# The first product of two feed forwards, by blocks in seven products instead of eight

## The chip, the cores and the metric

The kernel runs on one core of a Trainium2 chip. A time is the device time of one execution in microseconds (us). The kernel before took 2294.47 us (median of three runs, 2292.39 to 2301.81). The engines are named as in the profile: PE (TensorE: matrix products, with its weight loads as PEld), DVE (VectorE), ACT (ScalarE), POOL (GpSimd) and SP (SyncE, which here issues the transfers).

## The reference, cut to what matters

Two stacks of layers work on one array of 512 tokens by 1024 features in float32. The second stack has two layers, and each ends with a feed forward, which is all that the change touches:

```
h = rmsnorm(x, norm_g[i, 2]) * (1.0 + sc2) + sh2
y = jnp.square(jax.nn.relu(h @ ffn_w1[i])) @ ffn_w2[i]      # 1024 -> 4096 -> 1024
x = x + g2 * rmsnorm(y, norm_g[i, 3])
```

Layer 0 also has, beside its feed forward, to sum up the modulation (`c_act @ ada_w`) of layer 1.

## The kernel before

Float32 accuracy on PE comes from splitting. `split` (lines 191 and 192) writes a high part, rounded to fp32r, with a cast on ACT, and the rest with a subtraction on DVE; it reads two operands in SBUF there. `mm3` (lines 280 to 282) is then three matmuls: high by high, high by low, low by high. The transposed input of a feed forward lies in `XH` and `XL` (in the trace `xt_hi`, `xt_lo`): 8 blocks of 128 features by 512 tokens.

The 4096 hidden features are made in 8 chunks of 512. `up_first` makes chunk 0 in two halves of 256 tokens, as the tokens arrive. `up(c)` makes chunk c = 1 to 7: four weight pieces of 256 rows by 512 columns (2 KB per row), and for each of 4 groups of 128 features 8 times three matmuls of 512 columns, 96 in all. `act` takes each result through Relu and Square (ACT) and splits it into `H[c]`. `down(c)` multiplies two chunks with the second weight, 192 matmuls of 512 columns, and adds the result to `Y` (line 1290, DVE; for c = 0 a copy on ACT). The order is chunk 0, 1, down(0), 2, 3, down(2), 4, 5, down(4), 6, 7, and then `final_out` with the last two. So in each layer six chunks come in pairs (2, 3), (4, 5) and (6, 7), and chunk 1 comes right behind `up_first`.

The kernel is written with a layer that gives each engine its own list of instructions, sorted by a planner; an engine takes its list strictly in order. So an instruction that waits holds up all that stands behind it on its engine. Buffers come from two pools of slots: `mid` (4 KB per partition), divided into `w` for weights and `a` for the rest, and `small` (2 KB). A slot is given again in the order in which slots came free, so a transfer starts when the last reader of its slot is done. PSUM has 8 banks; `up` uses 0 to 3 for its four groups.

In the trace, POOL's only work near a feed forward is a power of a column (line 376), the reciprocal root that a block of 128 tokens needs twice: once when the residual is added, once when the new input is normed. The sums over `ada_w` (line 461) stand on DVE and wait for a transfer each.

Of the kernel before, what the change touches and what calls it, by code (L numbers as in the profile page):

```python
# [9 lines left out]
F32 = mybir.dt.float32  # L10
F32R = mybir.dt.float32r
# [5 lines left out]
P = 128  # L17
SEQ = 512
NB = SEQ // P
D = 1024  # L20
KD = D // P
# [9 lines left out]
def kernel(ctx: ExitStack, tc: tile.TileContext, inp: dict, out: bass.AP):  # L31
    nc = tc.nc
    V, S, G, T = nc.vector, nc.scalar, nc.gpsimd, nc.tensor
    mult, add, sub, amax, amin = ALU.mult, ALU.add, ALU.subtract, ALU.max, ALU.min
# [4 lines left out]
    class Ring:  # L39
        def __init__(self, items):  # L40
            self.items, self.i = items, 0
# [5 lines left out]
    def fixed(name, shape, dt=F32):  # L47
        return pool.tile([P] + list(shape), dt, tag=name, name=name)

    class Slots:  # L50
# [16 lines left out]
        def free(self, *tiles):  # L67
            for t in tiles:
                name, i = self.held.pop(t.name)
                self.idle[name].append(i)  # L70
# [14 lines left out]
    mid = Slots("mid", 4096, w=11, a=16)  # L85
    small = Slots("small", 2064, c=6, f=11, m=4)

    banks = [psum.tile([P, 512], F32, tag=f"bank{i}", name=f"bank{i}") for i in range(8)]
# [5 lines left out]
    XH = fixed("xt_hi", [KD, SEQ], F32R)  # L94
    XL = fixed("xt_lo", [KD, SEQ], F32R)
# [24 lines left out]
    def blk(i):  # L120
        return slice(i * P, (i + 1) * P)
# [67 lines left out]
    def split(hi, lo, src):  # L189

        S.copy(hi, src)  # L191
        V.tensor_sub(lo, src, hi.bitcast(F32))  # L192
# [4 lines left out]
    def w_piece(parts, nr=2):  # L197

        r, h, l = (mid.new("w", [nr, D // nr], dt) for dt in (F32, F32R, F32R))
        o = 0  # L200
        for ap in parts:
            n = ap.shape[1]
            nc.sync.dma_start(r[:, :, o : o + n], ap.rearrange("(k p) n -> p k n", p=P))
            o += n
        for i in range(nr) if by_tile[0] else (slice(0, nr),):
            split(h[:, i, :o], l[:, i, :o], r[:, i, :o])
        mid.free(r)
        return h, l
# [35 lines left out]
    class Turns:  # L244
# [18 lines left out]
        def need(self, key):  # L263

            while any(k == key for k, _, _ in self.steps):
                self.run()
# [12 lines left out]
    def mm3(o, lh, ll, rh, rl, start, stop):  # L279
        T.matmul(o, lhsT=lh, rhs=rh, start=start, stop=False)  # L280
        T.matmul(o, lhsT=lh, rhs=rl, start=False, stop=False)  # L281
        turns.passed(o, T.matmul(o, lhsT=ll, rhs=rh, start=False, stop=stop))  # L282
# [16 lines left out]
    def proj_feats(ws, ct, m=P, o=None, t=slice(0, SEQ)):  # L299

        if o is None:
            o = proj_bank.next()[:m, :]
        for k in range(KD):
            wh, wl = ws(k)
            mm3(o, wh[:, ct * P : ct * P + m], wl[:, ct * P : ct * P + m], XH[:, k, t], XL[:, k, t], k == 0, k == KD - 1)
        return o
# [4 lines left out]
    def dense(w, row0, nk, cols, term, tiles=(0, 1, 2, 3), nr=2):  # L311

        bs = {i: banks[n] for n, i in enumerate(tiles)}
        for k0 in range(0, nk, nr):
            r = slice(row0 + k0 * P, row0 + (k0 + nr) * P)
            h, l = w_piece([w[r, c0 : c0 + n] for c0, n in cols], nr)
            for i in tiles:
                for q in range(nr):
                    k = k0 + q
                    term(bs[i], i, k, h[:, q, :], l[:, q, :], k == 0, k == nk - 1)  # L320
            mid.free(h, l)
        return bs
# [7 lines left out]
    def of_out(o):  # L330
        return lambda b, tb, k, wh, wl, start, stop: mm3(b, *o(tb)(k), wh, wl, start, stop)

    def out_half(nk, o, ws):

        b = out_bank.next()
        for k in range(nk):
            mm3(b, *o(k), *ws(k), k == 0, k == nk - 1)
        return b

    def pair(name):  # L340

        t = mid.new(name, [2, 4, P], F32R)
        return t, t[:, 0, :, :], t[:, 1, :, :]
# [106 lines left out]
    def ada_sum(l, part):  # L450

        for k in range(KD):
            for hf in range(2):
                t = ada_in[0].next()
                c0 = part * D + hf * 512
                nc.sync.dma_start(t, inp["ada_w_2"][l, k * P : (k + 1) * P, c0 : c0 + 512])
                a, ck = ada_acc[hf], c_act[:, k : k + 1]
                if k == 0:
                    V.tensor_scalar(a, t, ck, None, op0=mult)
                else:  # L460
                    V.scalar_tensor_tensor(a, t, ck, a, op0=mult, op1=add)  # L461
# [756 lines left out]

    def final_out(o, w, row0, Y, row, then):

        acc = [tiny(2) for _ in range(NB)]
        ys = []
        for hf in range(2):
            ws = bs = None
            if hf == 0:
                bs = dense(w, row0, KD, [(0, 512)], of_out(o))
            else:
                ws = out_weight(w, row0, KD, hf)
            for tb in range(NB):
                b = out_half(KD, o(tb), ws) if ws else bs[tb]  # L1230
                if Y is None:
                    ys.append(small.new("f", [512]))
                    S.copy(ys[-1], b)
                else:
                    ys.append(Y[tb][hf])
                    V.tensor_add(ys[-1], ys[-1], b)
                mean_squares(acc[tb][:, hf : hf + 1], ys[-1], D)
                V.tensor_mul(ys[-1], ys[-1], row[hf])
                if hf == 1:
                    with tc.high_priority(100):  # L1240
                        res_block(tb, (ys[tb], ys[NB + tb]), acc[tb], row, then)
        ws.free()


    def ffn(l, then):
        w1, w2 = inp["ffn_w1_2"][l], inp["ffn_w2_2"][l]
        mid.share(w=15, a=12, front=True)
        small.share(c=6, f=11, front=True)
        H = {}

        def act(hi, lo, b, shape):
            t = small.new("c", [SEQ])
            S.activation(t, b, AF.Relu)
            S.activation(t, t, AF.Square)
            split(hi, lo, t.rearrange("p (c t) -> p c t", c=shape) if shape else t)
            small.free(t)

        def up(c):
            H[c] = Parts()
            bs = dense(w1, 0, KD, [(512 * c, 512)], by_feat)  # L1260
            for ct in range(4):
                act(H[c].hi[ct], H[c].lo[ct], bs[ct], None)

        def up_first():

            H[0] = Parts()
            ws = Weight(w1, 0, KD, [(0, 512)])
            for hf in range(2):
                need(2 * hf + 1)
                if hf:  # L1270
                    small.share(c=4, f=13)
                t = slice(hf * 256, hf * 256 + 256)
                for q in range(2):
                    b = proj_bank.next()
                    for i in range(2):
                        proj_feats(ws, 2 * q + i, o=b[:, i * 256 : i * 256 + 256], t=t)
                    act(H[0].hi.ts[q][:, :, t], H[0].lo.ts[q][:, :, t], b, 2)
            ws.free()

        def of(c, tb):  # L1280
            return lambda k: H[c + k // 4](k % 4, blk(tb))

        def down(c):
            for hf in range(2):
                bs = dense(w2, 512 * c, KD, [(512 * hf, 512)], of_out(lambda tb: of(c, tb)))
                for tb in range(NB):
                    if c == 0:
                        S.copy(Y[tb][hf], bs[tb])
                    else:
                        V.tensor_add(Y[tb][hf], Y[tb][hf], bs[tb])  # L1290
            H.pop(c).free()
            H.pop(c + 1).free()

        up_first()
        mid.share(w=15, a=12)
        Y = [[small.new("f", [512]) for _ in range(2)] for _ in range(NB)]
        up(1)
        ada_sum(l, 5)
        down(0)
        row = ada_row(l, 5)  # L1300
        parts = [0, 1, 3, 4] if l == 0 else []
        for c in range(2, 8):
            up(c)
            if parts and c > 2:
                ada_cols(1, parts.pop(0))
            if parts:
                ada_sum(1, parts[0])
            if c in (3, 5):
                down(c - 1)
        small.share(c=7, f=10)  # L1310
        final_out(lambda tb: of(6, tb), w2, 512 * 6, Y, row, then)
        for q in (H.pop(6), H.pop(7)):
            q.free()
        small.free(*row)
# [113 lines left out]
    ple(1, NextH(0, 0))  # L1428
    mlstm(NextH(0, 2))
    ffn(0, NextH(1, 0))  # L1430
    sgu(NextH(1, 2))
    ffn(1, Store())


# [31 lines left out]
```

## Time and profile before

| | us |
|---|---|
| median of three runs | 2294.47 |
| the profiled execution | 2298.11 |
| its span, first to last instruction | 2296.4 |
| PE busy | 2249.7 |
| DVE busy | 1290.5 |
| ACT busy | 923.8 |
| POOL busy | 101.1 |

The profile is one execution, 3.6 us above the median of the runs. Busy time is the union of an engine's instructions; a busy PE is not PE at its peak, because its matmuls overlap. What a matmul costs in a dense stretch is the distance from one start to the next: 192 matmuls of 512 columns stand in the 44.41 us from 2022.10 to 2066.51, which is 0.231 us each, though one matmul shows 0.39 us.

### The profile page before, as it was taken

Reading aid. Unit: us, or ns where it says so; the run is one execution under the profiler, and the core shown is the slowest. Engines: PE = TensorE matmul, PEld = TensorE weight load, DVE = VectorE, ACT = ScalarE, POOL = GpSimd, SP = SyncE. Lnnn points to the kernel's source line nnn. Section 1 sums busy time; section 2 is a strip of 40 time slices with the busy share of each in tenths; the row PEclk is TensorE's granted clock in tenths of the full one; section 3 lists DMA queues with packets and bytes.
Section 4 is the critical chain, followed back from the end, with each engine's and each line's share of the span. In section 5 each row is a group of like instructions: output and inputs, shape, how many; then the busy total and the mean of one; then the engine's idle time right before and its main releaser. Section 6 shows DMA issues by size and latency. Waiting matters only on the chain.

```text
span 2296.4 us, 27232 instructions
## 1 busy us (share of the span) xinstructions
PE 2249.7 (98%) x10248; PEld 1803.4 (79%) x10248; DVE 1290.5 (56%) x2466; ACT 923.8 (40%) x1728; POOL 101.1 (4%) x157
## 2 busy tenths in 40 slices
PE   8999999999999999999998999999999998999998
PEld 6787788787777777887777887778788887888887
DVE  5665755844895857843647525556646457323334
ACT  4333444334354544333445432414535234442423
POOL 0000000100000000100211000000002101000000
PEclk9999999999999999999999999999999999999999
DMA  5343434222222124224414625454233443332230
GB/s 171 111 136 103 144 91 132 84 61 65 85 72 74 37 88 158 77 66 124 154 50 143 194 92 165 147 184 147 65 120 107 127 149 109 120 100 92 92 101 37
DMA packets 145767, 251.03 MB, mean 109 GB/s; under 512 B 13787, under 2 KB 34483, under 8 KB 145635
## 3 DMA queue, kind: packets, MB, share of 16 engines
q1 hardware_dynamic: 145632, 249.29, 34.7%
q8 instruction: 80, 1.31, 0.2%
q14 instruction: 55, 0.43, 0.1%
HBM read 247.15 MB, written 2.10 MB: 109 GB/s over the span
## 4 chain that ended last, share of the span: by engine, by line
PE 84%; DVE 7%; DMA 5%; ACT 2%; issue 1%; POOL 1%; SPq 0%; DVEq 0%; POOLq 0%; ACTq 0%
PE bank L280 25%; PE bank L281 25%; PE bank L282 25%; DMA small<-in_ada_w_dram 4%; DVE small L461 2%; PE bank L988 2%; DVE mid L192 1%; PE bank L287 1%; POOL tiny_c L376 1%; PE bank L1167 1%; PE bank L1172 1%; PE bank L1003 1%; PE bank L1391 1%; DVE x_res L521 0%; DMA mid<-in_gla_w_in_dram 0%
## 5 line engine op out<-in xcount | busy, mean ns | idle before, releaser
L192 DVE TENSOR_TENSOR mid<-mid,mid 128x512 fp32r<-128x512 f32 (+2 forms) x488 | 437.6, 916 | 623.0 <-ACT mid L191 550.5
L191 ACT CAST mid<-mid 128x512 fp32r<-128x512 f32 (+2 forms) x488 | 377.6, 799 | 854.4 <-PE bank L282 307.7
L280 PE MATMUL bank<-xt_hi,mid 128*128 128x512 f32 (+1 forms) x1216 | 471.7, 389 | 10.7 <-ACT xt_hi L191 9.6
L281 PE MATMUL bank<-xt_lo,mid 128*128 128x512 f32 (+1 forms) x1216 | 469.8, 386 | 4.2 <-DVE xt_lo L192 4.2
L282 PE MATMUL bank<-xt_hi,mid 128*128 128x512 f32 (+1 forms) x1216 | 468.9, 386 | 0.0
L280 PE MATMUL bank<-mid,mid 128*128 128x512 f32 x1032 | 410.1, 397 | 2.7 <-DVE small L1290 1.2
L281 PE MATMUL bank<-mid,mid 128*128 128x512 f32 x1032 | 407.7, 395 | 0.0
L282 PE MATMUL bank<-mid,mid 128*128 128x512 f32 x1032 | 407.6, 395 | 0.0
L280 PEld LDWEIGHTS bank<-xt_hi,mid 128*128 128x128 f32 x1216 | 230.8, 190 | 62.6 <-ACT xt_hi L191 11.8
L281 PEld LDWEIGHTS bank<-xt_lo,mid 128*128 128x128 f32 x1216 | 231.3, 190 | 52.6 <-DVE xt_lo L192 5.2
L282 PEld LDWEIGHTS bank<-xt_hi,mid 128*128 128x128 f32 x1216 | 231.3, 190 | 49.1 <-issue 1.4
L280 PE MATMUL bank<-mid,xt_hi 128*128 128x512 f32 (+1 forms) x640 | 252.5, 395 | 0.8 <-ACT mid L191 0.8
L282 PE MATMUL bank<-mid,xt_lo 128*128 128x512 f32 (+1 forms) x640 | 250.4, 391 | 1.0 <-DVE xt_lo L192 0.9
L281 PE MATMUL bank<-mid,xt_hi 128*128 128x512 f32 (+1 forms) x640 | 250.3, 391 | 0.4 <-DVE mid L192 0.4
L280 PEld LDWEIGHTS bank<-mid,mid 128*128 128x128 f32 x1032 | 194.0, 188 | 49.0 <-DVE small L1290 2.1
L282 PEld LDWEIGHTS bank<-mid,mid 128*128 128x128 f32 x1032 | 193.9, 188 | 44.7
L281 PEld LDWEIGHTS bank<-mid,mid 128*128 128x128 f32 x1032 | 193.9, 188 | 44.0 <-issue 0.5
L461 DVE SCALAR_TENSOR_TENSOR small<-small,c_act,small 128x512 f32<-128x512 f32 x168 | 123.5, 749 | 78.8 <-DMA small<-in_ada_w_dram 77.9
L282 PEld LDWEIGHTS bank<-mid,xt_lo 128*128 128x128 f32 x640 | 120.6, 188 | 28.3 <-DVE xt_lo L192 1.9
L280 PEld LDWEIGHTS bank<-mid,xt_hi 128*128 128x128 f32 x640 | 120.7, 189 | 26.3 <-ACT mid L191 1.2
L281 PEld LDWEIGHTS bank<-mid,xt_hi 128*128 128x128 f32 x640 | 120.6, 188 | 26.2 <-DVE mid L192 0.9
L192 DVE TENSOR_TENSOR mid<-small,mid 128x512 fp32r<-128x512 f32 (+1 forms) x125 | 85.8, 689 | 55.3 <-ACT mid L191 54.9
(276 smaller groups left out, 2029.5 us busy)
## 6 DMA issues: line engine op xcount, KB each, us to landing
mid<-in_ffn_w_dram SPq DMA_DIRECT2D x128, 512.0 KB, 3.6
small<-in_ada_w_dram SPq DMA_DIRECT2D x192, 256.0 KB, 3.2
mid<-in_dsa_w_in_dram SPq DMA_DIRECT2D x36, 512.0 KB, 3.5
mid<-in_gla_w_in_dram SPq DMA_DIRECT2D x32, 512.0 KB, 4.3
mid<-in_b_w_in_dram SPq DMA_DIRECT2D x32, 512.0 KB, 3.7
mid<-in_a_w_in_dram SPq DMA_DIRECT2D x24, 512.0 KB, 3.9
mid<-in_gla_w_in_dram SPq DMA_DIRECT2D x32, 256.0 KB, 3.0
mid<-in_gla_w_out_dram SPq DMA_DIRECT2D x16, 512.0 KB, 3.8
```

Of the source, the lines that this page charges most:

```text
L191: S.copy(hi, src)
L192: V.tensor_sub(lo, src, hi.bitcast(F32))
L280: T.matmul(o, lhsT=lh, rhs=rh, start=start, stop=False)
L281: T.matmul(o, lhsT=lh, rhs=rl, start=False, stop=False)
L282: turns.passed(o, T.matmul(o, lhsT=ll, rhs=rh, start=False, stop=stop))
L287: i = T.transpose(b[:, blk(c)], src, ident)
L376: G.tensor_tensor(r, v, minus_half[:, 0:m], op=ALU.pow)
L461: V.scalar_tensor_tensor(a, t, ck, a, op0=mult, op1=add)
L988: T.matmul(b[:, :n], lhsT=QT[tb][:, blk(c)], rhs=KT[:, :n], start=True, stop=True)
L1003: T.transpose(b[:, blk(c)], es[c][:, blk(j)], ident)
L1167: T.matmul(sb[:, :n], lhsT=KT[pr, c // 2, blk(j)], rhs=QT[pr, c // 2, j * P :], start=True, stop=True)
L1172: T.matmul(nb[i // 2][:, (i % 2) * 129 : (i % 2) * 129 + 129], lhsT=Dm[j][:, blk(i - j)], rhs=vv[j][:, c, :], start=j == 0, stop=j == i)
```

## The change

`up(c)` for c = 1 to 7 no longer runs 96 matmuls of 512 columns. The product of a chunk is cut into blocks, 2 by 2 on both sides: the input by halves of the features and halves of the tokens, the weight by halves of its rows and of its columns (1 KB per row). Seven products of sums of blocks then stand for eight, each of 24 matmuls of 256 columns (2 groups of 128 features, 4 blocks of features, three matmuls), 168 in all.

- The sums of input blocks are made once per layer (`Sums`): two on POOL over `XL`, eight on DVE, and four splits. The fourth sum overwrites the block of `XH` and `XL` that nothing needs any more.
- The sums of weight blocks are made for each chunk (`seven`): four subtractions of 128x1024 on POOL, each from the one before, and seven splits of 128x1024 (before: four).
- The products are put together with seven additions of 128x512 on DVE, which read a PSUM bank each, and one copy on ACT. Relu now reads SBUF. The product with `s1` is needed twice and stays in its bank until line 425.
- The seven banks come from a ring of six, 0 to 5. In the pool `mid`, `w` goes from 15 to 13 slots and `a` from 12 to 14 (six are held by the sums); before `final_out`, `w` gets 19.

```
+        b11, b12, b22, b21 = load(0, c0), load(0, c1), load(1, c1), load(1, c0)
+        p = parts(b11)
+        G.tensor_tensor(b12, b12, b11, op=sub)
+        m1, u = small.new("c", [512]), small.new("c", [512])
+        S.copy(m1, product("11", p))
+        t2 = mid.new("w", [4, 256])
+        G.tensor_tensor(t2, b22, b12, op=sub)
+        p = parts(b12)
+        mid.free(b12)
+        p5 = product("s1", p)
+        p = parts(t2)
+        G.tensor_tensor(b11, t2, b11, op=sub)
+        V.tensor_add(u, product("s2", p), m1)
+        c12 = small.new("c", [512])
+        V.tensor_add(c12, u, p5)
+        p = parts(b21)
+        G.tensor_tensor(t2, b21, t2, op=sub)
+        mid.free(b21)
+        V.tensor_add(m1, m1, product("12", p))
+        done(0, 0, m1)
+        p = parts(b11)
+        mid.free(b11)
+        V.tensor_add(u, u, product("s3", p))
+        c22 = small.new("c", [512])
+        V.tensor_add(c22, u, p5)
+        done(1, 1, c22)
+        p = parts(t2)
+        mid.free(t2)
+        V.tensor_add(u, u, product("22", p))
+        done(1, 0, u)
+        p = parts(b22)
+        mid.free(b22)
+        V.tensor_add(c12, c12, product("s4", p))
+        done(0, 1, c12)
...
         def up(c):
             H[c] = Parts()
-            bs = dense(w1, 0, KD, [(512 * c, 512)], by_feat)
-            for ct in range(4):
-                act(H[c].hi[ct], H[c].lo[ct], bs[ct], None)
+            seven(w1, 512 * c, 512 * c + 256, sums, done)
...
-        mid.share(w=15, a=12)
+        mid.share(w=13, a=14)
         Y = [[small.new("f", [512]) for _ in range(2)] for _ in range(NB)]
+        sums = Sums()
         up(1)
```

In `Sums`, `hf` and `lf` are the blocks of `XH` and `XL`, and `s1`, `s2`, `s3` are float32 scratch:

```
+            G.tensor_tensor(s2, lf[1][0], lf[1][1], op=add)
+            V.tensor_add(s1, hf[1][0], hf[1][1])
+            V.tensor_add(s1, s1, s2)
+            split(*s[0], s1)
+            G.tensor_tensor(s3, lf[0][0], lf[1][0], op=sub)
+            V.tensor_sub(s2, s1, hf[0][0])
+            V.tensor_sub(s2, s2, lf[0][0])
+            split(*s[1], s2)
+            V.tensor_sub(s1, hf[0][0], hf[1][0])
+            V.tensor_add(s3, s3, s1)
+            split(*s[2], s3)
+            V.tensor_sub(s1, hf[0][1], s2)
+            V.tensor_add(s1, s1, lf[0][1])
+            split(h[1][0], l[1][0], s1)
```

The lines behind the change are 96 higher in the new kernel: 496, 497 and 376 of the old one are 592, 593 and 472 of the new. DVE's list in layer 0, from the last parts of `XL` on, which stand just ahead of these rows in both kernels. Before (`mid_647` is a low part of `H[0]`, line 461 the sums over `ada_w`):

```order
L192 TENSOR_TENSOR mid_648_9600<-small_413_9766,mid_646_9598 128x2x256
L497 TENSOR_TENSOR small_428_10309<-small_428_10309,small_429_10310 128x512
L496 TENSOR_TENSOR small_430_10316<-small_430_10316,bank7_68 128x512
L459 TENSOR_SCALAR small_357_8232<-small_359_8234,c_act_144 128x512
L497 TENSOR_TENSOR small_430_10316<-small_430_10316,small_431_10317 128x512
L461 SCALAR_TENSOR_TENSOR small_356_8231<-small_358_8233,c_act_144,small_356_8231 128x512
```

Now (`mid_667`, `mid_668` and `mid_669` are the scratch s1, s2 and s3, `mid_662` and `mid_664` the low parts of the first two sums, `mid_679` that of the first weight block):

```order
L356 TENSOR_TENSOR mid_667_9891<-xt_hi_70 128x1024
L593 TENSOR_TENSOR small_428_10433<-small_428_10433,small_429_10434 128x512
L357 TENSOR_TENSOR mid_667_9891<-mid_667_9891,mid_668_9892 128x1024
L592 TENSOR_TENSOR small_430_10440<-small_430_10440,bank7_68 128x512
L360 TENSOR_TENSOR mid_668_9892<-mid_667_9891,xt_hi_70 128x1024
L192 TENSOR_TENSOR mid_662_9886<-mid_667_9891,mid_661_9885 128x1024
L361 TENSOR_TENSOR mid_668_9892<-mid_668_9892,xt_lo_71 128x1024
L192 TENSOR_TENSOR mid_647_9599<-small_414_9819,mid_645_9597 128x2x256
L363 TENSOR_TENSOR mid_667_9891<-xt_hi_70 128x1024
L192 TENSOR_TENSOR mid_664_9888<-mid_668_9892,mid_663_9887 128x1024
L364 TENSOR_TENSOR mid_669_9893<-mid_669_9893,mid_667_9891 128x1024
L192 TENSOR_TENSOR mid_679_9925<-mid_674_9916,mid_678_9924 128x1024
```

Six sums and two of their splits now stand ahead of the first split of the chunk's weight, and the sums over `ada_w` have moved behind them. On PE, at the end of `up_first` and the start of chunk 1, before (`mid_666`, `mid_667` are the first weight piece):

```order
L280 MATMUL bank0_61<-xt_hi_70,mid_666_9890 128x512
L281 MATMUL bank0_61<-xt_lo_71,mid_666_9890 128x512
L282 MATMUL bank0_61<-xt_hi_70,mid_667_9891 128x512
L280 MATMUL bank0_61<-xt_hi_70,mid_666_9890 128x512
L281 MATMUL bank0_61<-xt_lo_71,mid_666_9890 128x512
```

Now (`mid_678`, `mid_679` are the parts of the first weight block, `mid_681` and `mid_683` high parts of the next two):

```order
L280 MATMUL bank0_61<-xt_hi_70,mid_678_9924 128x256
L281 MATMUL bank0_61<-xt_lo_71,mid_678_9924 128x256
L280 MATMUL bank2_63<-mid_663_9887,mid_683_9986 128x256
L281 MATMUL bank2_63<-mid_664_9888,mid_683_9986 128x256
L280 MATMUL bank1_62<-mid_661_9885,mid_681_9958 128x256
L281 MATMUL bank1_62<-mid_662_9886,mid_681_9958 128x256
L282 MATMUL bank0_61<-xt_hi_70,mid_679_9925 128x256
L280 MATMUL bank0_61<-xt_hi_70,mid_678_9924 128x256
```

Four matmuls of the second and third product now stand in the first, so that these products' parts are needed there. The third place is DVE in layer 1 at the passage from chunk 2 to chunk 3. Before (`mid_1169` to `mid_1180` are the four weight pieces of chunk 3 and their parts, `mid_1151` and `mid_1152` low parts of `H[2]`):

```order
L192 TENSOR_TENSOR mid_1171_15655<-mid_1169_15653,mid_1170_15654 128x1024
L192 TENSOR_TENSOR mid_1174_15685<-mid_1172_15683,mid_1173_15684 128x1024
L192 TENSOR_TENSOR mid_1177_15715<-mid_1175_15713,mid_1176_15714 128x1024
L192 TENSOR_TENSOR mid_1180_15745<-mid_1178_15743,mid_1179_15744 128x1024
L192 TENSOR_TENSOR mid_1151_15507<-small_584_15629,mid_1149_15505 128x512
L192 TENSOR_TENSOR mid_1151_15507<-small_585_15634,mid_1149_15505 128x512
L192 TENSOR_TENSOR mid_1152_15508<-small_586_15639,mid_1150_15506 128x512
```

Now (lines 423, 425, 429 and 433 are additions of chunk 2's products; `mid_1199`, `mid_1202`, `mid_1204` and `mid_1206` the low parts of chunk 3's first four weight blocks, `mid_1169` and `mid_1170` those of `H[2]`):

```order
L192 TENSOR_TENSOR mid_1199_16053<-mid_1194_16044,mid_1198_16052 128x1024
L423 TENSOR_TENSOR small_577_15817<-small_577_15817,bank0_61 128x512
L192 TENSOR_TENSOR mid_1169_15801<-small_576_15816,mid_1167_15799 128x2x256
L425 TENSOR_TENSOR small_579_15968<-small_577_15817,bank3_64 128x512
L192 TENSOR_TENSOR mid_1202_16087<-mid_1195_16046,mid_1201_16086 128x1024
L429 TENSOR_TENSOR small_577_15817<-small_577_15817,bank1_62 128x512
L192 TENSOR_TENSOR mid_1204_16115<-mid_1200_16084,mid_1203_16114 128x1024
L433 TENSOR_TENSOR small_578_15903<-small_578_15903,bank2_63 128x512
L192 TENSOR_TENSOR mid_1170_15802<-small_579_15968,mid_1168_15800 128x2x256
L192 TENSOR_TENSOR mid_1206_16147<-mid_1197_16050,mid_1205_16146 128x1024
```

All splits of chunk 3's weight stood ahead of the low parts of `H[2]`; now they alternate with additions that wait for chunk 2's products, and each chunk has seven of either. POOL's list, which held only the powers of a column here, now has the first weight sum of chunk 1 (line 403) between the powers of the third and the fourth block of tokens, and then lines 359, 355, 407, 412 and 417.

## Rows read from the trace of the kernel before

**Rows 1.** The page: span, busy time of each engine, and the chain that ended last.

```profile
span 2296.4 us, 27232 instructions
...
PE 2249.7 (98%) x10248; PEld 1803.4 (79%) x10248; DVE 1290.5 (56%) x2466; ACT 923.8 (40%) x1728; POOL 101.1 (4%) x157
...
PE 84%; DVE 7%; DMA 5%; ACT 2%; issue 1%; POOL 1%; SPq 0%; DVEq 0%; POOLq 0%; ACTq 0%
```

**Rows 2.** Windows: chunk 1 of layer 0, and a later stretch.

```profile
core 0: us, PE busy (x) PEld busy (x) DVE busy (x) ACT busy (x) POOL busy (x), PEclk, DMA share, GB/s
1280.46:1302.24 21.78, 21.78 (x96) 17.68 (x95) 13.44 (x17) 10.87 (x15) 0.00 (x0) 1.00 0.79 265
2022.10:2066.51 44.41, 44.41 (x193) 36.10 (x192) 13.18 (x13) 19.18 (x29) 0.00 (x0) 1.00 0.30 95
```

**Rows 3.** Timeline of PE: start, us, line, out<-in, shape. First of 93 intervals, and their end.

```profile
1269.45 0.28 PE L282 MATMUL bank<-xt_hi,mid 128*128 128x256 f32 x1
...
1280.46 0.40 PE L280 MATMUL bank<-xt_hi,mid 128*128 128x512 f32 x1
```

**Rows 4.** Groups by line and form: busy, mean ns | idle before, releaser.

```profile
L192 DVE TENSOR_TENSOR mid<-mid,mid 128x1024 fp32r<-128x1024 f32 x208 | 255.9, 1232 | 452.3 <-ACT mid L191 451.3 <-issue 0.7
L191 ACT CAST mid<-mid 128x1024 fp32r<-128x1024 f32 x208 | 217.4, 1047 | 537.7 <-PE bank L282 216.4 <-PE bank L281 203.4 <-DMA mid<-in_b_w_in_dram 55.1
```

**Rows 5.** Timeline of DVE and POOL, each with the other idle.

```profile
1286.02 2.36 DVE L192 TENSOR_TENSOR mid<-mid,mid 128x1024 fp32r<-128x1024 f32 x2 [0.38 <-ACT mid L191]
1268.49 1.29 DVE L192 TENSOR_TENSOR xt_lo<-small,xt_hi 128x512 fp32r<-128x512 f32 x2
1269.69 0.69 DVE L192 TENSOR_TENSOR mid<-small,mid 128x512 fp32r<-128x512 f32 x1
1783.69 5.18 POOL L1372 TENSOR_TENSOR mid<-mid,small 128x512 f32<-128x512 f32 x4 [21.50 <-DMA small<-in_b_ln_b_dram]
```

**Rows 6.** Timeline of DVE and POOL where both work at once.

```profile
1809.53 2.35 DVE L192 TENSOR_TENSOR mid<-mid,mid 128x1024 fp32r<-128x1024 f32 x1 [1.74 <-ACT mid L191]
1809.51 4.76 POOL L1372 TENSOR_TENSOR mid<-mid,small 128x512 f32<-128x512 f32 x3 [20.65 <-DMA small<-in_b_ln_b_dram]
1178.34 1.01 POOL L376 TENSOR_TENSOR tiny_c<-tiny_c,minus_half 128x4 f32<-128x4 f32 x1 [6.50 <-DVE tiny_c L1182]
1178.35 0.69 DVE L1168 TENSOR_TENSOR small<-small,bank 128x512 f32<-128x512 f32 x1
```

**Rows 7.** Timeline of SP, POOL and PE where layer 0's tokens arrive.

```profile
1242.25 0.38 SPq L203 DMA_DIRECT2D mid<-in_ffn_w_dram  x1
...
1246.49 1.46 POOL L376 TENSOR_TENSOR tiny_c<-tiny_c,minus_half 128x1 f32<-128x1 f32 x1 [3.99 <-DVE tiny_c L388]
1249.07 0.55 POOL L376 TENSOR_TENSOR tiny_c<-tiny_c,minus_half 128x1 f32<-128x1 f32 x1 [1.12 <-DVE tiny_c L388]
...
1247.91 0.50 PE L280 MATMUL bank<-xt_hi,mid 128*128 128x256 f32 x2 [3.20 <-ACT xt_hi L191]
1251.06 0.58 PE L281 MATMUL bank<-xt_lo,mid 128*128 128x256 f32 x1 [2.65 <-DVE xt_lo L192]
```

**Rows 8.** The page: issues, KB each, median us from issue to landing.

```profile
mid<-in_a_w_in_dram SPq DMA_DIRECT2D x24, 512.0 KB, 3.9
```

**Rows 9.** Waits in 1483 to 1533 us: total, times, longest.

```profile
PE bank L470 <- DVE small L461: 3.1, 1, 3.1
```

**Rows 10.** Windows (columns as in rows 2) of both spells at the lower clock.

```profile
1248.54:1255.37 6.83, 4.31 (x20) 4.31 (x21) 6.76 (x11) 3.28 (x7) 0.55 (x1) 0.50 0.37 97
1920.97:1931.21 10.24, 5.51 (x24) 5.22 (x25) 9.36 (x16) 5.69 (x12) 1.85 (x2) 0.50 0.19 53
```

**Rows 11.** Timeline of PE ahead of the second spell.

```profile
1924.12 0.58 PE L280 MATMUL bank<-xt_hi,mid 128*128 128x256 f32 x1 [5.39 <-ACT xt_hi L191]
```

More of the change, by code (lines that the diff above doesn't have):

```diff
@@ L338, in out_half, with __init__, blocks, free @@
         return b
+    seven_bank = Ring(banks[0:6])
+    class Sums:
+        def __init__(self):
+            def blocks(t):
+                return [[t[:, 4 * h : 4 * h + 4, 256 * i : 256 * i + 256] for h in range(2)] for i in range(2)]
+            h, l = blocks(XH), blocks(XL)
+            hf, lf = ([[b.bitcast(F32) for b in r] for r in m] for m in (h, l))
+            s = [[mid.new("a", [4, 256], F32R) for _ in range(2)] for _ in range(3)]
+            s1, s2, s3 = (mid.new("a", [4, 256]) for _ in range(3))
+            G.tensor_tensor(s2, lf[1][0], lf[1][1], op=add)
[12 more added lines that the diff above has]
+            split(h[1][0], l[1][0], s1)
+            mid.free(s1, s2, s3)
+            self.held = [t for p in s for t in p]
+            self.of = {"11": (h[0][0], l[0][0]), "12": (h[0][1], l[0][1]), "22": (h[1][1], l[1][1])}
+            self.of.update({f"s{i + 1}": s[i] for i in range(3)}, s4=(h[1][0], l[1][0]))
+        def free(self):
+            mid.free(*self.held)
@@ new lines, in seven, with load, parts, product @@
+    def seven(w, c0, c1, left, done):
+        def load(h, c):
+            r = mid.new("w", [4, 256])
+            nc.sync.dma_start(r, w[4 * h * P : 4 * (h + 1) * P, c : c + 256].rearrange("(k p) n -> p k n", p=P))
+            return r
+        def parts(r):
+            h, l = (mid.new("w", [4, 256], F32R) for _ in range(2))
+            split(h, l, r)
+            return h, l
+        def product(at, right):
+            b = seven_bank.next()
+            for c in range(2):
+                for k in range(4):
+                    lh, ll = (t[:, k, blk(c)] for t in right)
+                    rh, rl = (t[:, k, :] for t in left.of[at])
+                    mm3(b[:, 256 * c : 256 * c + 256], lh, ll, rh, rl, k == 0, k == 3)
+            mid.free(*right)
+            return b
+        b11, b12, b22, b21 = load(0, c0), load(0, c1), load(1, c1), load(1, c0)
[32 more added lines that the diff above has]
+        done(0, 1, c12)
@@ L1249, in ffn, with act @@
         H = {}
-        def act(hi, lo, b, shape):
-            t = small.new("c", [SEQ])
+        def act(hi, lo, b, shape, t=None):
+            if t is None:
+                t = small.new("c", [SEQ])
             S.activation(t, b, AF.Relu)
@@ L1259, in up, with done @@
             H[c] = Parts()
-            bs = dense(w1, 0, KD, [(512 * c, 512)], by_feat)
-            for ct in range(4):
-                act(H[c].hi[ct], H[c].lo[ct], bs[ct], None)
+            def done(t, n, src):
+                at = slice(256 * t, 256 * t + 256)
+                act(H[c].hi.ts[n][:, :, at], H[c].lo.ts[n][:, :, at], src, 2, src)
+            seven(w1, 512 * c, 512 * c + 256, sums, done)
         def up_first():
@@ L1309, in ffn @@
                 down(c - 1)
+        sums.free()
+        mid.share(w=19, a=8)
         small.share(c=7, f=10)
```

## The prediction

> **What bounds the kernel now.** I read the page first: the busy time of the engines and the chain that ended last. The reader is to see there that PE is busy for 98% of the span, that 84% of the chain is PE, and that POOL is nearly idle [rows 1]. So what PE is spared is time gained, as long as the parts that it multiplies come in time, and the second view to read is the stretch itself, by windows: in chunk 1 of layer 0 PE runs 96 matmuls in 21.78 us without a pause, DVE works 13.4 and POOL not at all [rows 2]. The third is the timeline where a changed operation, or one like it, stands: for its price alone, and for its price beside another engine [rows 3 to 6]. Last come the places where PE does wait near the change: the arrival of a layer's tokens, the transfers and sums ahead of it, and the clock behind such waits [rows 7 to 11].
>
> **The change part by part.** The sum is made against the profiled execution, 2298.1 us (its span of 2296.4 and 1.7 around it), which is 3.6 above the median.
>
> *PE's matmuls.* A matmul of 512 columns costs 44.41 / 192 = 0.231 us from start to start [rows 2], so an `up` of 96 costs 22.2. Matmuls of 256 columns stand at the end of `up_first`: 93 intervals from 1269.45 to 1280.46, 0.1184 each [rows 3], a little over half. Seven products of 24 are 168 x 0.1184 = 19.9 (2.84 each). So seven eighths of the columns give 0.90 of the time: 2.29 us less per `up`, and for 14 of them **-32.0**.
>
> *What the other engines get.* A DVE operation of 128x1024 on two SBUF operands costs 2.36 for two, less the overlap of their ends: 1.14 from start to start; one of 512 costs 0.60 (1268.49 to 1269.69 for two) [rows 5]. ACT's cast of 1024 takes 1.05 [rows 4]. POOL's nearest operation is of 128x512, 5.18 for four, 1.3 each [rows 5]; at twice the size I take 2.5. What decides is whether POOL and DVE work at once. At 1809.5 they start together: DVE's split takes 2.35 in place of 1.14, one POOL operation longer, and POOL's three take 4.76, about 1 us over what three take alone [rows 6]. So they take turns when DVE reads two operands in SBUF. A DVE operation that reads one operand from a bank took 0.69 beside POOL, no longer than alone [rows 6]. I take it that the splits and the sums exclude POOL, and that the additions from banks don't.
>
> Per `up`, DVE has 7 splits of 1024 and 11 operations of 512 (seven additions from banks, four low parts): 8.0 + 6.6 = 14.6, ACT about the same, POOL 10. Each fits below 19.9; DVE and POOL in turns, 24.6, don't.
>
> *Chunk 1 of each layer.* Time zero is the end of the last low parts of the tokens, 1270.3 [rows 5]; PE ends `up_first` at 1280.46, +10.2 [rows 3]. DVE's list up to the first weight block's split has nine operations of 1024 and three of 512: 12.1. POOL has lines 355 and 407 meanwhile, 2 x 2.5 in turns with them: the split is done at 17.1. PE runs a few matmuls on the high parts before and waits 6.5. The second block's split stands four operations of 1024, one of 512 and POOL's line 412 further, 7.7: at 24.8. PE is done with the 22 matmuls left of the first product at 19.7 and waits 5.1. The other 140 take 16.6, and the fourth split, behind line 417, costs 0.7 more: it ends at 42.1, against 10.2 + 19.9 = 30.1 without a wait. That is 12.0 per layer, **+24.0**. Bounds: if POOL and DVE didn't exclude each other, the splits come at 12.1 and 17.3, and 4.5 per layer is lost (9); if two more POOL operations come in between, 17 (34). I take 24, by the row at 1809.5, which is the same kind of operation.
>
> *Line 403 in front of a power.* POOL's list has the first weight sum between the powers of the third and the fourth block of tokens. Its data come by a transfer whose slot the issue at 1242.25 has now, and land 3.9 later [rows 7, 8], near 1246.2; POOL works on it from about 1248 to 1250.5, exactly where the last power stood (1249.07), and where PE waits 2.65 for low parts [rows 7]. DVE's splits there take turns with it. Loss 0 to 2.5 per layer, I take 2: **+4.0** (0 to 5).
>
> The Trainium skill, SBUF — State Buffer, "Who interferes with whom", says that a VectorE instruction with at most one SBUF operand doesn't contend with GpSimd unless it runs in a 2-port mode, such as an fp32 `tensor_scalar` from SBUF to SBUF may; then the other engine is shut out for the whole instruction. The two rows at 1809.5 and 1178.3 agree with its first half; no row here shows POOL beside such an operation. By it the norm's `tensor_scalar` (line 506 before) would wait for line 403 too, and this term would be 5 in place of 4.
>
> *Pairs of chunks.* The first `up` of a pair has its weights, POOL's sums and three splits done during the `down` before it, where DVE works 13.2 of 44.4 us [rows 2]: no loss. It is the second, B, that is tight. With A's start at zero: `w` has 13 slots, and B's first two blocks get theirs when A's third product ends, 8.5; they land at 12.4 [rows 8]. Line 403 to 15.0, B's first split 16.2, line 407 to 18.7, a low part of `H` 19.3, and then DVE reaches line 425 of A, which frees the bank that B's first product needs: 19.9, just when PE comes. Line 412 to 21.8, second split 22.9 (needed at 22.7), third 24.7, line 417 to 27.2, fourth 29.0 (needed at 28.4). So 0.6 per pair for five; layer 0's pair (4, 5) has the sums over `ada_w` queued on DVE ahead of the fourth split, 3.3: **+6.3**. Bounds: 0 if turns cost less than I take, 28 by a rival below.
>
> *The clock.* Waits of 3.2 and 2.65 in layer 0 and of 5.39 in layer 1 were followed by 6.83 and 10.24 us at a granted clock of 0.50, that is 1.2 GHz [rows 7, 10, 11]. Chunk 1's first wait is as long. But PE waits a second time in most of such a spell, so little is lost by it: **+3.0** for both layers (0 to 10, half of each spell).
>
> *At nothing:* the transfers (1 KB rows cost 3.9 for 512 KB at 30% share of DMA [rows 2, 8]; if late, a rival); the two POOL sums over `XL`, whose cost is in chunk 1; `final_out` with more slots. Layer 0's `down(4)` waits 3.1 for the sums over `ada_w` now [rows 9]; PE comes later, so up to 3 may come back, which I leave out.
>
> Sum: -32.0 + 24.0 + 4.0 + 6.3 + 3.0 = +5.3: 2303.4 profiled, **2300** at the median.
>
> **Rivals.** *Hidden sums, faster.* POOL and DVE overlap after all, or the planner's list leaves DVE early enough: chunk 1 loses 9, the rest nothing, -23: 2271. For it: DVE is idle 44% of the span [rows 1]. Against: the row at 1809.5.
>
> *Every second `up` bound by DVE and POOL, slower.* The place is line 425 and the second split in B. In turns the two need 24.6 per chunk, and PE 19.9. It decides as soon as line 425 comes after 19.9, and my margin there is nil: a late bank makes A's end late, and B's splits behind it. Then each pair loses 4.7, six of them 28 in place of 6.3: 2322. For it: the row at 1809.5, and a list without slack. Against: a long `down` in front lets the first `up`'s work be done ahead.
>
> *Weights late.* B's last two blocks come only after A's fourth product, and POOL's chain, each sum from the one before, adds to 3.9 of transfer: 1 us per pair, 2306.
>
> That the change doesn't do what it says would be 256 columns costing more than half of 512: at 0.132 the gain is nil. The 93 intervals speak against it, and I give it nothing of its own.
>
> **How the numbers follow.** My forecast has 0.44, with 2289 to 2309 as its own range; hidden sums 0.20; B bound 0.29; weights late 0.07. About 0.5%, 11.5 us, is what a measurement of this kernel can tell from no change: faster is below 2283, slower above 2306. Faster gets 0.20 and 0.02 from the edge of my own case; slower 0.29, half of the weights' 0.07 and 0.05 from my own; the rest, 0.40, is the same. The range leaves out a tenth on either side: half of each outer case, 2276 to 2324, which takes in the 9 of the lower bound in chunk 1 and the 28 of the upper one in the pairs.
>
> **What would show it.** Right: in both layers two waits of PE in chunk 1, 6.5 and 5 us, ahead of matmuls on `mid` parts and released by DVE's split; DVE operations of 1024 that take 2 to 3.6 us there; POOL operations of 1024 at 2.5 and its busy time up by 60 x 2.5 = 150 us; first `up`s of pairs at 19.9, second ones at 20.5. Wrong: PE without waits in chunk 1; a spacing of 256 columns other than 0.118; second `up`s at 22 or more; a spell at half clock in each pair.

## The result, and the profile after

The changed kernel takes 2329.57 us (median of four runs, 2326.77 to 2333.02) against 2296.11 of the kernel before: 1.0144 times as long, 95% interval 1.0117 to 1.0171. So it is slower by 33.5 us, 1.4%; the forecast was 5.3 slower, and its range ended at 2324.

The page of the changed kernel, against [rows 1]:

```profile
span 2324.9 us, 29691 instructions
...
PE 2231.3 (96%) x11256; PEld 1840.7 (79%) x11256; DVE 1487.8 (64%) x2630; ACT 982.0 (42%) x1792; POOL 268.4 (12%) x217
...
PE 71%; DVE 11%; DMA 8%; issue 4%; ACT 3%; POOL 2%; SPq 0%; DVEq 0%; POOLq 0%; ACTq 0%
```

PE has less to do and is busy 18 us less, but holds only 71% of the chain in place of 84. Next to read are the stages of the two feed forwards, by the times at which PE goes from one to the next (us; the last column is e3, an experiment below with all sums on DVE):

| stage | layer 0 before | after | layer 1 before | after | e3, layers 0 / 1 |
|---|---|---|---|---|---|
| PE's wait for the tokens, chunks 0 and 1 | 58.6 | 75.5 | 59.0 | 76.9 | 64.1 / 65.6 |
| down(0) | 44.4 | 44.7 | 44.4 | 46.8 | 44.5 / 44.9 |
| chunks 2, 3 | 45.4 | 40.5 | 44.4 | 39.9 | 40.5 / 39.8 |
| down(2) | 45.6 | 46.2 | 44.6 | 44.6 | 44.6 / 44.6 |
| chunks 4, 5 | 45.5 | 43.7 | 44.4 | 40.1 | 45.6 / 39.7 |
| down(4) | 50.2 | 55.5 | 44.4 | 44.5 | 46.6 / 44.5 |
| chunks 6, 7 | 45.6 | 46.4 | 44.5 | 41.2 | 40.6 / 39.9 |
| the last two chunks' second product | 46.2 | 55.2 | 44.2 | 44.2 | 48.9 / 44.3 |
| sum | 381.4 | 407.6 | 370.0 | 378.2 | 375.4 / 363.3 |

The layers lose 26.2 and 8.2, 34.5 in all. The spans differ by 28.5 only, because the stages ahead of layer 0 took 6.1 us longer in the profiled execution of before, though nothing was changed there (PE is done ahead of the tokens at 1243.68 before, 1237.62 after).

So layer 1's pairs gain about what was forecast (some 12 of 133), the stage up to the end of chunk 1 loses 16.9 and 17.9, and layer 0 loses on top of that, late. First a pair of layer 1 and its `down`, by windows (columns as in rows 2), in the kernel after:

```profile
2062.74:2102.59 39.85, 39.85 (x336) 39.85 (x337) 31.38 (x31) 23.52 (x33) 10.12 (x4) 1.00 0.34 104
2102.59:2147.20 44.61, 44.61 (x195) 36.05 (x194) 20.49 (x21) 13.06 (x16) 9.60 (x4) 1.00 0.31 98
```

These are 336 matmuls without a pause, 0.1186 each. DVE and POOL stand at 31.4 + 10.1 here, 41.5 in a stage of 39.9, and PE loses nothing: busy times hold the time in which the two hold each other up, and the additions that read a bank run beside POOL. Now the same kernel in layer 0, chunks 4 and 5 to the end:

```profile
1444.55:1488.25 43.70, 41.40 (x345) 40.78 (x343) 32.91 (x39) 19.90 (x27) 12.15 (x5) 1.00 0.37 115
1488.25:1543.72 55.47, 47.90 (x200) 38.31 (x201) 38.88 (x47) 17.18 (x22) 7.57 (x3) 0.94 0.60 193
1543.72:1590.07 46.35, 41.78 (x345) 40.77 (x344) 42.81 (x48) 22.55 (x31) 13.56 (x5) 1.00 0.42 134
1590.07:1645.22 55.15, 49.85 (x208) 39.86 (x209) 37.98 (x57) 24.43 (x47) 3.88 (x5) 0.94 0.45 147
```

In chunks 6 and 7 DVE is busy 42.8 of 46.4, and the clock falls in both `down`s. What PE waits for there, 1488 to 1646 (waits as in rows 9):

```profile
PE bank L566 <- DVE small L557: 6.8, 1, 6.8
PE bank L280 <- DVE small L433: 3.1, 1, 3.1
PE bank L282 <- DVE mid L192: 2.6, 3, 1.5
```

These, the longest, are DVE come late: the last sum over `ada_w` (line 557 now), the last addition of chunk 7, and splits. Around the first of them POOL is idle, from 1486 to 1512, so there it is not POOL that holds DVE. Part of the delay is in the transfers. SP issues the feed forward's weights and the parts of `ada_w` from one list, in order; it waited 16.9 us with one of `ada_w`, until 1474.79, and weights of `down(4)` stood behind it. ACT waited for such a weight, and DVE then stood idle 3.38 us for ACT (waits of SP in 1440 to 1515, then ACT's cast):

```profile
SPq L552 <- DVE mod_cols L579: 16.9, 1, 16.9
```

```profile
1487.15 1.05 ACT L191 CAST mid<-mid 128x1024 fp32r<-128x1024 f32 x1 [10.72 <-DMA mid<-in_ffn_w_dram]
```

Chunk 1 of layer 0: PE's waits, then DVE, ACT and POOL (start, us), and the two spells at half clock by windows:

```profile
1282.56 0.58 PE L280 MATMUL bank<-mid,mid 128*128 128x256 f32 x1 [5.98 <-ACT mid L191]
1284.74 0.58 PE L282 MATMUL bank<-xt_hi,mid 128*128 128x256 f32 x1 [0.88 <-DVE mid L192]
1294.29 0.58 PE L280 MATMUL bank<-mid,mid 128*128 128x256 f32 x1 [4.45 <-ACT mid L191]
```

```profile
1275.00 3.40 DVE L192 TENSOR_TENSOR mid<-mid,mid 128x1024 fp32r<-128x1024 f32 x1
1284.61 1.21 DVE L366 TENSOR_TENSOR mid<-xt_hi,mid 128x1024 f32<-128x1024 f32 x1
1285.74 1.21 DVE L192 TENSOR_TENSOR mid<-mid,mid 128x1024 fp32r<-128x1024 f32 x1
1286.88 0.68 DVE L192 TENSOR_TENSOR mid<-small,mid 128x512 fp32r<-128x512 f32 x1
1287.48 1.21 DVE L367 TENSOR_TENSOR mid<-mid,xt_lo 128x1024 f32<-128x1024 f32 x1
1288.62 2.35 DVE L192 TENSOR_TENSOR mid<-mid,mid 128x1024 fp32r<-128x1024 f32 x2
...
1293.19 1.04 ACT L191 CAST mid<-mid 128x1024 fp32r<-128x1024 f32 x1 [6.58 <-POOL mid L412]
...
1274.36 2.96 POOL L407 TENSOR_TENSOR mid<-mid,mid 128x1024 f32<-128x1024 f32 x1 [3.84 <-issue]
1284.91 8.25 POOL L412 TENSOR_TENSOR mid<-mid,mid 128x1024 f32<-128x1024 f32 x1 [7.59 <-DVE mid L192]
```

```profile
1279.01:1289.25 10.24, 5.80 (x25) 5.51 (x26) 10.24 (x11) 6.47 (x8) 4.34 (x1) 0.50 0.00 0
1292.66:1299.49 6.83, 5.20 (x24) 5.20 (x25) 3.50 (x3) 3.48 (x4) 2.86 (x2) 0.50 0.01 2
```

Line 412 begins at 1284.91 and is held as long as DVE works without a pause, to 1290.97; then it takes 2.2. ACT's cast at 1293.19 waits for its result, and PE's wait of 4.45 ends with that cast. Elsewhere DVE is the one that waits: the split at 1275.00 takes 3.40, behind line 407.

### The profile page after: what moved, and what is told of

Its sections match the earlier page's. It is cut to its first block, busy times and chain, and to the rows that moved or that the text cites. A ratio compares the mean times of both kernels' runs of the same rounds, so it can differ in the third digit from the quotient of the medians.

```text
span 2324.9 us, 29691 instructions
## 1 busy us (share of the span) xinstructions
PE 2231.3 (96%) x11256; PEld 1840.7 (79%) x11256; DVE 1487.8 (64%) x2630; ACT 982.0 (42%) x1792; POOL 268.4 (12%) x217
## 3 DMA queue, kind: packets, MB, share of 16 engines
q1 hardware_dynamic: 159968, 249.29, 34.5%
## 4 chain that ended last, share of the span: by engine, by line
PE 71%; DVE 11%; DMA 8%; issue 4%; ACT 3%; POOL 2%; SPq 0%; DVEq 0%; POOLq 0%; ACTq 0%
PE bank L280 21%; PE bank L281 21%; PE bank L282 21%; DMA small<-in_ada_w_dram 5%; DVE mid L192 3%; DMA mid<-in_ffn_w_dram 2%; DVE small L557 2%; ACT mid L191 2%; PE bank L1084 2%; PE bank L287 1%; PE bank L1263 1%; POOL tiny_c L472 1%; PE bank L1099 1%; PE bank L1268 1%; POOL mid L412 1%
## 5 line engine op out<-in xcount | busy, mean ns | idle before, releaser
L192 DVE TENSOR_TENSOR mid<-mid,mid 128x512 fp32r<-128x512 f32 (+2 forms) x536 | 520.4, 991 | 484.6 <-ACT mid L191 315.3
L191 ACT CAST mid<-mid 128x512 fp32r<-128x512 f32 (+2 forms) x536 | 426.3, 821 | 811.8 <-DMA mid<-in_ffn_w_dram 170.5
L280 PE MATMUL bank<-mid,mid 128*128 128x512 f32 (+1 forms) x1368 | 510.5, 373 | 32.7 <-ACT mid L191 22.5
L281 PE MATMUL bank<-mid,mid 128*128 128x512 f32 (+1 forms) x1368 | 506.5, 370 | 0.8 <-DVE mid L192 0.8
L282 PE MATMUL bank<-mid,mid 128*128 128x512 f32 (+1 forms) x1368 | 505.4, 370 | 0.2 <-DVE mid L192 0.2
L280 PE MATMUL bank<-xt_hi,mid 128*128 128x512 f32 (+1 forms) x1216 | 424.0, 349 | 15.2 <-ACT xt_hi L191 11.1
L281 PE MATMUL bank<-xt_lo,mid 128*128 128x512 f32 (+1 forms) x1216 | 421.1, 347 | 7.7 <-DVE xt_lo L192 7.7
L282 PE MATMUL bank<-xt_hi,mid 128*128 128x512 f32 (+1 forms) x1216 | 420.7, 346 | 5.4 <-DVE mid L192 5.4
L280 PEld LDWEIGHTS bank<-mid,mid 128*128 128x128 f32 x1368 | 260.9, 191 | 82.4 <-ACT mid L191 24.2
L281 PEld LDWEIGHTS bank<-mid,mid 128*128 128x128 f32 x1368 | 261.4, 191 | 45.1 <-DVE mid L192 1.2
L282 PEld LDWEIGHTS bank<-mid,mid 128*128 128x128 f32 x1368 | 260.5, 191 | 45.4 <-DVE mid L192 0.4
L280 PEld LDWEIGHTS bank<-xt_hi,mid 128*128 128x128 f32 x1216 | 233.5, 192 | 48.2 <-ACT xt_hi L191 13.2
L282 PEld LDWEIGHTS bank<-xt_hi,mid 128*128 128x128 f32 x1216 | 233.5, 192 | 35.5 <-DVE mid L192 6.6
L557 DVE SCALAR_TENSOR_TENSOR small<-small,c_act,small 128x512 f32<-128x512 f32 x168 | 132.4, 802 | 63.1 <-DMA small<-in_ada_w_dram 61.9
L280 PEld LDWEIGHTS bank<-mid,xt_hi 128*128 128x128 f32 x640 | 120.7, 189 | 26.2 <-ACT mid L191 1.2
L472 POOL TENSOR_TENSOR tiny_c<-tiny_c,minus_half 128x1 f32<-128x1 f32 (+1 forms) x68 | 52.9, 779 | 741.2 <-DVE tiny_c L486 375.7
```

What stands on the lines that cost most here:

```text
L472: G.tensor_tensor(r, v, minus_half[:, 0:m], op=ALU.pow)
```

## The experiments

**e1_chunk1_dense.** Chunk 1 by the old code (`up_old` is the `up` of before), the sums of input blocks between the halves of `down(0)`, their scratch from `w`:

```
+        up_old(1)
+        mid.share(w=13, a=14)
+        down(0, lambda: sums.append(Sums()))
```

> Chunk 1 of each layer runs as before (96 matmuls of 512 columns); the sums of input blocks are made in the middle of down(0), chunks 2 to 7 run by seven products. Theory A (what chunk 1 loses is the wait for the sums ahead of its first split, and the half clock behind it): the 16.8 us of layer 0 and the 17.6 + 2.4 of layer 1 go, 2293, and up to 6 more if the sums delay down(0)'s weights. Rival C (13 slots for weights in place of 15, later loads): the slots are as in the changed kernel, chunk 1 is a small part, so no better than 2320.

2292.67 us, 0.9979 of before (0.9956 to 1.0003): no different from the kernel before, and 37 us of the changed kernel's time hang on chunk 1, as theory A has it. Rival C doesn't fall by this run alone: its edit gives chunk 1 back its 15 slots and takes the scratch from `w`. It falls with e3 below, which gets 47.6 us back with the slots of the changed kernel.

**e2_layer1_pairs.** Layer 0 wholly by the old code, layer 1 as in e1:

```
-            up(c)
+            (up if l else up_old)(c)
```

> Seven products only for chunks 2 to 7 of layer 1, all else as before; 13 slots there. Theory A (matmuls of 256 columns give what was forecast, and where DVE has no sums over ada_w the pairs hide the rest): about 12 us below the kernel before, 2284, or up to 3 more if the sums delay down(0). Rival C (slots): no gain, 2296 or above.

2285.72 us, 0.9959 (0.9942 to 0.9976): 10 faster. The seven products are worth what the spacing of 256 columns said where nothing else fills DVE. Between e1 and e2 lies layer 0: its pairs by seven products cost about 7 us in place of a gain of 14. That 7 is rough, since the ten runs of e1 go from 2283.89 to 2301.89.

**e5_no_ada_sums.** The kernel leaves out four parts of the sums over `ada_w`, and their transfers, inside layer 0's feed forward. A fifth part, which the next block needs (line 1506), stays, and falls into chunks 6 and 7 and the last stage:

```
-                ada_sum(1, parts[0])
+                pass
```

> Layer 0's feed forward leaves out the loads and sums over ada_w for layer 1's modulation (four parts of 16 operations on DVE); all else as the changed kernel. Theory A (layer 0's pairs lose 22 us because DVE has these sums beside seven's work): layer 0's chunks 2 to 7 take the times of layer 1's, 22 us less and the 3 that the kernel before waits for the same sums: 2304. Rival B (POOL alone): the pairs lose as before, only the 3 to 7 us wait for the last sum goes: 2323.

2309.93 us, 1.0069 (1.0044 to 1.0094): 19.6 below the changed kernel, of 25 expected. Layer 0's chunks 4 to the end, against the windows above:

```profile
1445.35:1485.62 40.27, 40.27 (x342) 40.22 (x340) 32.06 (x33) 24.36 (x34) 10.58 (x4) 1.00 0.32 105
1485.62:1532.62 47.00, 45.20 (x199) 36.47 (x198) 21.43 (x23) 12.77 (x16) 9.60 (x4) 1.00 0.28 90
1532.62:1575.57 42.95, 41.08 (x346) 40.69 (x344) 33.94 (x38) 21.64 (x29) 10.54 (x4) 1.00 0.35 114
1575.57:1627.90 52.33, 48.25 (x209) 38.68 (x209) 38.39 (x57) 25.26 (x49) 3.89 (x5) 0.97 0.48 159
```

Chunks 4 and 5 run at full speed, 40.3. The last stage stays 6 too long: PE waits 3.8 there for the last addition of chunk 7, which DVE has behind splits. No sum over `ada_w` stands in that wait, but 11 of the fifth part stand in the stage. The run leaves out sums and transfers together, so it doesn't part the time of the sums on DVE from the weights that wait on SP behind those transfers.

**e3_sums_on_dve.** Every sum on VectorE, nothing else changed; one of six like edits:

```
-        G.tensor_tensor(b12, b12, b11, op=sub)
+        V.tensor_tensor(b12, b12, b11, op=sub)
```

> All sums on VectorE in place of GpSimd, same order of emission. Theory A and rival B (POOL's turns are what fills DVE): each sum costs DVE 1.14 in place of a turn of 2.5. Chunk 1's splits come at 14.4 and 20.7 in place of 17.1 and 24.8, 4 us less wait per layer and less half clock; layer 0's pairs have 5.4 less per chunk on DVE: in all about 2308. If turns with POOL are rare outside chunk 1, DVE is 4.6 per chunk fuller and layer 0's pairs lose 10 more: 2335.

2281.99 us, 0.9950 (0.9934 to 0.9966): faster than before, and 47.6 below the changed kernel, twice what was expected. By the table, 23 of it are the stages up to the end of chunk 1 in both layers, where 4 per layer and some half clock were expected, and 21 the rest of layer 0. Its page, and chunk 1 of layer 0 by windows, then its only long wait:

```profile
span 2279.9 us, 29583 instructions
...
PE 2218.7 (97%) x11256; PEld 1831.5 (80%) x11256; DVE 1490.1 (65%) x2690; ACT 981.1 (43%) x1792; POOL 103.1 (5%) x157
```

```profile
1274.76:1302.34 27.58, 21.38 (x167) 21.14 (x167) 27.42 (x29) 16.44 (x22) 0.00 (x0) 0.94 0.21 73
```

```profile
1284.40 0.58 PE L280 MATMUL bank<-mid,mid 128*128 128x256 f32 x1 [5.39 <-ACT mid L191]
```

The telling number is DVE's: 60 more operations, and 1490.1 us busy against 1487.8. Having POOL do the sums spared DVE next to nothing. Chunk 1 is bound by DVE in e3, 27.4 of 27.6.

**e6_pool_beside.** e3, and POOL works beside it for nothing:

```
+        G.tensor_tensor(b12, b12, b12, op=sub)
         mid.free(b12)
```

(so for `b21`, `b11` and `t2`, each where it is freed).

> All sums on VectorE as in e3_sums_on_dve, and beside them GpSimd does four subtractions of 128x1024 per chunk in buffers whose content nothing needs any more; no one waits for their result, only the slots come free later by their length. If the loss is that POOL and DVE take turns (DVE's splits stretched by 2.4 each time), chunk 1 loses 5 to 7 per layer again and layer 0's pairs most of their 22: 2305 to 2320. If it is only that a sum takes 2.5 on POOL in place of 1.14 in a chain that PE waits for, nothing comes back: 2282 to 2286.

2318.03 us, 1.0092 (1.0063 to 1.0122): 36 us come back by operations whose result no one reads. Splits of 128x1024 in three kernels, first the changed one, then e3, then e6 (columns as in rows 4):

```profile
L192 DVE TENSOR_TENSOR mid<-mid,mid 128x1024 fp32r<-128x1024 f32 x256 | 338.8, 1332 | 318.3 <-ACT mid L191 220.4 <-PE bank L282 74.8 <-PE bank L281 19.8
```

```profile
L192 DVE TENSOR_TENSOR mid<-mid,mid 128x1024 fp32r<-128x1024 f32 x256 | 312.8, 1227 | 265.9 <-ACT mid L191 206.4 <-PE bank L282 45.7 <-PE bank L281 12.8
```

```profile
L192 DVE TENSOR_TENSOR mid<-mid,mid 128x1024 fp32r<-128x1024 f32 x256 | 350.1, 1375 | 259.5 <-ACT mid L191 209.8 <-PE bank L282 38.6 <-PE bank L281 6.1
```

e6 holds slots longer too; but ACT's waits for the feed forward's weights in layer 0 (1230 to 1650 us) are no longer, e3 first:

```profile
ACT mid L191 <- DMA mid<-in_ffn_w_dram: 84.8, 20, 8.3
```

```profile
ACT mid L191 <- DMA mid<-in_ffn_w_dram: 82.0, 17, 8.9
```

By stages, e6 against e3, and in brackets the changed kernel against e3: up to the end of chunk 1, 1.0 and 3.0 us in the two layers (11.4 and 11.3); the rest of layer 0, 23.1 (20.8); the rest of layer 1, 9.7 (3.6). So behind chunk 1, POOL's work beside DVE is enough for the loss, without a sum of POOL's in the chain that PE waits for. Chunk 1 is another matter: the 5 to 7 us per layer that were expected did not come back. There the loss hangs on POOL's sums standing in that chain, which e6 doesn't have: lines 359, 355 and 407, behind which DVE's operations stretch ahead of the first weight's split, and line 412, for which ACT's cast waits. That much is read from the trace of the changed kernel; no run moves these four alone. So it is partly luck that e6 gives back so much of the 47.6.

**e7_dve_chunk1_dense.** e1 and e3 together.

> Chunk 1 as before in both layers (e1_chunk1_dense) and all sums on VectorE (e3_sums_on_dve). If the two losses are apart: 2282 less what chunk 1 still loses there by its stretches, 5.5 in layer 0 and 6.7 in layer 1: 2270, or up to 5 more if the sums in the middle of down(0) delay its weights. If e3's gain was mostly chunk 1's, no better than 2280.

2272.83 us, 0.9893 (0.9869 to 0.9918): faster than both kernels, 23.9 below the one before, and 3 above what was expected: what e3 still loses in chunk 1 and what it gained elsewhere are apart. What is missing of the ideal, 12 x 2.3 = 27, lies in layer 0, whose chunks 4 and 5 take 45.1 us and whose last stage takes 48.1. POOL has no sum there, so this is not its doing; the parts of `ada_w` are still in it.

## Why the prediction was wrong

By its own terms, in the two profiled executions:

| term | forecast | measured | from |
|---|---|---|---|
| matmuls | -32.0 | -32 | layer 1's pairs: 39.85 for 44.4 |
| chunk 1, PE's waits | +24.0 | +21.8 | 5.98 + 0.88 + 4.45, and 10.4 in layer 1 |
| line 403 ahead of a power | +4.0 | +4.4 | PE's two waits for the tokens, against before |
| the clock | +3.0 | +13.4 | by difference: what chunks 0 and 1 lose beside these waits |
| pairs | +6.3 | +24.3 | 22.7 of it in layer 0, chunks 2 to the end |
| down(0) | 0 | +2.7 | the table |
| sum | +5.3 | +34.6 | |

**The matmuls** came out as their spacing in the trace of before [rows 3]: 0.1186 against 0.1184.

**The step that failed first: the pairs.** The prediction put it as "0.6 per pair for five", and 3.3 for layer 0's pair (4, 5). The walk was good for layer 1, which loses 1.6 in three pairs. In layer 0 it counted the sums over `ada_w` once, as a queue in front of one split. They are 16 operations per part, 14 of them on two operands in SBUF, and they fall mostly into the stages behind the pairs, which should do work ahead: 4 of line 557 stand in chunks 4 and 5, 21 in `down(4)`, 6 in chunks 6 and 7 and 11 in the last stage. They take DVE's time there and stretch beside POOL (their mean is 802 ns, 748 in e3), and their transfers stand ahead of weights on SP. The windows above give the budget that I should have drawn up for them: over the four stages DVE is busy 152.6 us and POOL 37.2, 189.8 of 200.7; in layer 1 the same sum for a pair and its `down` is 71.6 of 84.5. Both hold the time of mutual waits, so they show how full the two are and not why; in e3 DVE does POOL's sums as well and is busy 149.0 of 181.8. The rival "every second `up` bound by DVE and POOL" had the kind of loss right, but not the place: of the 22.7 us, 14.9 lie in the products behind the pairs and 7.8 in the pairs, all in layer 0 and not at its line 425. That its 2322 is nearer than my 2300 is in good part luck. e5 shows the sums over `ada_w`, with their transfers, as one half of the cause, e3 and e6 POOL as the other: from chunk 2 to the end of layer 0, e5 gets 19.7 us back and e3 20.5, so either taken away takes most of it.

The prediction's 24.6 us "in turns" also counted the seven additions from banks, which by its own reading of rows 6 don't exclude POOL; without them it is 20.4, hardly above PE's 19.9, and layer 1 shows that it fits.

**The clock** was mis-sized. I expected PE to wait through the slow spell. It fell at 1279.01, in the first wait, and stayed at 0.50 for 10.24 us, in which the first product ran; the second wait brought 6.83 more, in which PE did not wait but for the first 1.6. 6.0 us in layer 0 and 7.4 in layer 1 are what remains when waits and gain are taken off the first row of the table; the spell at the arrival of the tokens, which is in it, grew as well, from 6.83 to 10.24 in layer 0 and from 10.24 to 13.65 in layer 1. In e3 one wait of 5.39 was left and the clock of its chunk 1 was 0.94 on the mean.

**Chunk 1's waits** were right in size, and by a mechanism that was half wrong. "In turns" holds for one operation against one. Line 412, reckoned at 2.5, took 8.25: POOL got no turn there between operations of DVE that followed without a pause. The second wait was no longer than forecast also because the first product ran at half clock meanwhile, and so ended later.

**Line 403** cost about what I said, at another place. It ran at 1241.09, which is 1247.2 by the clock of the execution before (6.1 earlier here), one us sooner than I put it, and so beside the norm of the third block of tokens instead of ahead of the fourth one's power. The norm's two operations took 0.88 before; in the changed kernel, DVE, then POOL:

```profile
1241.16 2.96 DVE L602 TENSOR_SCALAR small<-x_res,tiny_c 128x512 f32<-128x512 f32 x2 [0.66 <-POOL tiny_c L472]
...
1241.09 2.35 POOL L403 TENSOR_TENSOR mid<-mid,mid 128x1024 f32<-128x1024 f32 x1
```

PE's waits were 4.37 and 3.44 in place of 3.20 and 2.65 [rows 7]. The first began before line 403 ran and is 4.21 in e3 too, so it is another matter; the second is 1.65 in e3, and in layer 1 it is 3.65 against 1.57, which makes 3.9 for both layers. The Trainium skill, SBUF — State Buffer, "Who interferes with whom", says that `tensor_scalar` can run in a 2-port mode, and that whichever of it and a GpSimd operation issues first then shuts the other out; the trace agrees, 2.57 for the first of the two operations, behind a line 403 that began just before it.

**At nothing:** the transfers of 1 KB rows (line 383) land in 4.0 us at the median in the kernel after, and the slots didn't decide (e3). The 2.7 in `down(0)` I had not counted: DVE comes out of chunk 1 late (in layer 1, PE waits 0.8 for its last addition).

What stays open: how much of the last stage of layer 0 (48.1 in the best kernel, 46.2 before) is the order of DVE's list, since no kernel was run with another order there; and how much of layer 0's loss is the transfers of `ada_w` ahead of the weights on SP, since e5 took them away together with the sums.

## What to carry to other kernels

Work moved to GpSimd is no relief for VectorE when that works on two operands in SBUF: here its 60 sums on GpSimd stretched VectorE's other operations by some 66 us (an estimate: 60 times 1.14, less the 2.3 by which the two busy times differ), as much as VectorE takes for them itself. So add both engines' time against PE's, over each pair of chunks and its `down`, with everything else that stands there. A cheaper product earns what its spacing says only where its preparation can be done ahead; the first chunk behind a barrier, with nothing to hide the sums, is better left as it was. And PE's waits in chunk 1, of 4.3 to 6 us, are to be priced with the half clock that came with them, here 6.83 to 10.24 us for each (3.41 in layer 0 of e3).

## What the runs showed of the hardware

- POOL is held by an unbroken run of DVE operations on two SBUF operands: 8.25 us (alone 2.4) in chunk 1 of either layer, and in e6 8.43, where it ended only behind the first operation that reads a bank. e6's DVE, then POOL:

```profile
1283.10 1.21 DVE L192 TENSOR_TENSOR xt_lo<-mid,xt_hi 128x1024 fp32r<-128x1024 f32 x1
...
1288.78 1.21 DVE L192 TENSOR_TENSOR mid<-mid,mid 128x1024 fp32r<-128x1024 f32 x1
1289.91 0.68 DVE L596 TENSOR_TENSOR small<-small,bank 128x512 f32<-128x512 f32 x1
...
1283.31 8.43 POOL L409 TENSOR_TENSOR mid<-mid 128x1024 f32<-128x1024 f32 x1 [33.65 <-DVE mid L192]
```

- At other places POOL came in behind a single such operation (line 407 at 1274.36, with the next split taking 3.40). What tells the two apart is open.
- The additions that read a bank kept their 0.68 to 0.69 beside POOL throughout.
